# A two-layer streaming encoder on one core: S5 quarters, attention pairs and projections of the first mixer in one interleaved order, with the accumulator's memory lent to attention

## The chip, the cores and the metric

The kernel runs on one core of a Trainium2 chip, as one program. The time is device microseconds (us) of one execution. TensorE (PE in the profile, with PEld for its weight loads), VectorE (DVE), ScalarE (ACT) and GpSimd (POOL) compute; SyncE (SP) issues nearly all transfers.

## The reference, cut to what matters

Two requests are served in one step: 512 new frames of one stream, and 16 frames of each of 8 running streams, 640 rows of width 1024 in all. Two layers follow one another. Each has a half-weighted SwiGLU feed-forward part (FFN), a mixer and a second FFN, and after each of them a layer norm of ALPHA * x + sublayer(x). The change touches the first layer's mixer alone:

```python
proj = x @ w_in                      # (640 x 1024) @ (1024 x 2048): u | q | k | v, 512 columns each
ys, h_last = s5_recurrence(u, h0, a_bar, b_bar, c_mat)     # 32 groups, complex diagonal state of 64
y = ys + d_skip * u
g = gelu(y)
s5_out = g * sigmoid(g @ w_glu + b_glu)
# stick-breaking attention, 8 heads of 64, for each block of 128 queries
z = q @ k.T * 64 ** -0.5
sp = where(mask, softplus(z), 0)
w = where(mask, exp(log_sigmoid(z) - (reverse_cumsum(sp) - sp)), 0)
sb_out = w @ v
out = concatenate([s5_out, sb_out]) @ w_out
```

The 512 rows of the new stream attend causally to themselves. The 16 rows of each running stream attend to 256 cached keys and values and to their own rows. k, v and the last S5 states are outputs too.

## The kernel before, in words

The kernel is written in a framework that plans the order of each engine's instructions itself. Program order gives priorities; an instruction is put on its engine's queue when a plan with estimated durations says that its inputs and its buffer are ready, and so later work of the program can be queued between earlier work. Each queue then runs strictly in the planned order. Buffers come from pools with a fixed number of slots (`bufs`); pools of a closed block give their memory to those of the next.

All 640 columns of x, transposed, stand in SBUF as the sum of two parts, xh and xl, and every weight matrix is split in the same way when it arrives (`load_w` L106, `split` L94 and L95: a cast on ScalarE and a subtraction on VectorE). A product is three matmuls for each 128 rows of depth (`mm3`, L127). Weights are held in 11 units of 128 x 1024 fp32 (`UNITS`), two units for a load of 512 KB, behind four raw tiles that the DMAs fill. `yacc` (128 x 5 x 1024 fp32) is the residual accumulator: it holds x, and the projections out of FFN and mixer are added to it.

`mixer0` (from L604) runs in this order:

- u: four weights, eight column groups (`cm_proj`), copied to `g_` (L629).
- four S5 quarters (`s5_quarter`, L646 to L753): 128 of the 512 channels each. The tables m2, tt, et and rot come by DMA into buffers of their own; u is transposed twice (L661, L668), multiplied into the state inputs (L676), rotated and scanned on VectorE (L684 to L724), multiplied out (L730 with tt, L735 with et), transposed back (L743), and goes through a GELU made of exponentials (L748 to L753). The quarters use the four PSUM banks "b".
- v: four weights, five row tiles (L764), on the four banks "a".
- Then the block of S5 closes, and that of attention opens with new PSUM pools: three banks "a" for projections, one bank "o", and two tiles "z" of two banks each. `in_qk(p)` makes q and k of two heads (L932).
- Four pairs of heads. `attend(p, i)` works on query block i of 128 rows and its 128 (i + 1) keys, both heads in one z tile: scores (L838), mask (L841), softplus in four steps (clamp L827, two activations L82, maximum L830), a reverse running sum by a scan per head (L846), a subtraction (L848), an exponential (L82), transposes back into z (L853), a copy (L854) and the product with v into bank "o" (L857), which is copied over q at the end of the pair (L942). `sample(p)` does the running streams of that pair in one z tile and one bank "o" (L866 to L920), with cached keys and values by DMA (L883, L904).
- GLU of the S5 part (L963 to L966), the first half of the output projection (`out_half(0, t)`, L779, into yacc), and the second half with the layer norm, whose inputs are the attention results.

## Time and profile before

| | before |
|---|---|
| times of three runs | 2612.27, 2610.0, 2612.27 us, median 2612.27 |
| profiled execution, its own time | 2612.16 us |
| its span, first to last instruction | 2610.0 us |
| mean granted TensorE clock | 0.992 |
| busy in the span: PE, PEld, DVE, ACT, POOL | 2550.6, 2311.2, 2026.8, 1149.1, 239.2 us |
| S5 quarters | first transposes 483.3 us, first of the fourth quarter 532.0 us |
| v copied out of PSUM | 498.0 to 550.3 us (begin of the first and the last) |
| attention scores (L838) | 579.3 to 712.9 us (begin of the first and the last) |
| first half of the output added into yacc | from 671.1 us |

A line of the profile names the engine, the program line, the operation, what is written and read, the shape and the count, then busy time and mean duration of one, and after the second bar the idle time of the engine before it with what ended it. In the timeline the first two numbers are start and duration in us, and the bracket holds idle time before. In the table by stretches each engine has its busy time and its number of instructions; PEclk is the granted clock as a share of full speed. Ends of matmuls are modelled, so the ends of neighbours overlap by a fraction of a microsecond.

### The profile page before, as it was taken

What the parts mean: (1) busy time and instruction counts of PE and PEld (TensorE: products, weight loads), DVE (VectorE), ACT (ScalarE), POOL (GpSimd) and SP (SyncE); (2) the same over time, 40 slices, a digit from 0 to 9 for tenths busy, and PEclk for the clock granted to TensorE, in tenths of its full rate; (3) what the DMA queues carried; (4) which work ended last, traced back from release to release, by engine and by line L of the source; (5) the groups of instructions that cost most, each with busy time, mean ns of one, the idle gap of its engine ahead of it and who ended that gap; (6) DMA issues with size and microseconds to landing.
All of it is one profiled execution on the core that took longest, in us unless ns stands there. A gap on an engine that the chain in (4) does not pass through costs nothing. (4 is left out here: it accounts for less than half of the span.)

```text
span 2610.0 us, 41343 instructions
## 1 busy us (share of the span) xinstructions
PE 2550.6 (98%) x15673; PEld 2311.2 (89%) x15673; DVE 2026.8 (78%) x4074; ACT 1149.1 (44%) x2400; POOL 239.2 (9%) x356
## 2 busy tenths in 40 slices
PE   9999999999879999999999999999999999999998
PEld 8999999887559999999999999889989878898887
DVE  7898888667859777768976677877786789887778
ACT  4444444346524344334433343566565553343332
POOL 0000003010020000003000001311111150000001
PEclk9999999999979999999999999999999999999999
DMA  5233234542302232222222222456564622443432
GB/s 180 97 114 99 96 110 139 175 146 84 109 24 74 81 97 98 73 85 86 75 88 81 71 91 99 128 171 195 154 208 136 217 92 94 146 151 127 132 122 93
DMA packets 165751, 302.79 MB, mean 116 GB/s; under 512 B 19072, under 2 KB 89856, under 8 KB 165040
## 3 DMA queue, kind: packets, MB, share of 16 engines
q1 hardware_dynamic: 163792, 293.83, 35.0%
q0 software_dynamic: 1760, 6.33, 0.7%
q8 instruction: 123, 2.02, 0.3%
q14 instruction: 76, 0.62, 0.1%
HBM read 259.56 MB, written 40.54 MB: 115 GB/s over the span
## 5 line engine op out<-in xcount | busy, mean ns | idle before, releaser
L127 PE MATMUL bank<-w,h 128*128 128x512 f32 x2640 | 610.9, 391 | 0.0
L127 PEld LDWEIGHTS bank<-w,h 128*128 128x128 f32 x2640 | 492.5, 188 | 105.3 <-issue 3.4
L127 PE MATMUL bank<-xhi,w 128*128 128x256 f32 (+2 forms) x2528 | 556.6, 311 | 8.8 <-ACT w L94 5.7
L95 DVE TENSOR_TENSOR w<-raw,w 128x512 fp32r<-128x512 f32 x693 | 472.0, 692 | 101.9 <-ACT w L94 99.5
L340 PE MATMUL bank<-xhi,w 128*128 128x320 f32 x2432 | 540.1, 310 | 0.7 <-DVE w L95 0.3
L94 ACT CAST w<-raw 128x512 fp32r<-128x512 f32 x693 | 422.3, 620 | 254.8 <-PE bank L340 131.0
L127 PEld LDWEIGHTS bank<-xhi,w 128*128 128x128 f32 x2528 | 421.0, 188 | 21.7 <-issue 7.2
L340 PE MATMUL bank<-T,w 128*128 128x320 f32 x2736 | 425.6, 309 | 0.1
L340 PEld LDWEIGHTS bank<-xhi,w 128*128 128x128 f32 x2432 | 406.6, 188 | 7.1 <-issue 3.9
L340 PEld LDWEIGHTS bank<-T,w 128*128 128x128 f32 x2736 | 406.6, 188 | 0.4 <-DVE w L95 0.3
L127 PE MATMUL bank<-xlo,w 128*128 128x256 f32 (+2 forms) x1264 | 391.4, 310 | 1.7 <-DVE xlo L95 1.6
L340 PE MATMUL bank<-xlo,w 128*128 128x320 f32 x1216 | 375.5, 309 | 0.0
L94 ACT CAST w<-sw 128x512 fp32r<-128x512 f32 x228 | 137.8, 620 | 457.9 <-PE bank L127 276.7
L204 DVE SCALAR_TENSOR_TENSOR yacc<-bank,yacc 128x512 f32<-128x512 f32 x240 | 164.7, 688 | 213.6 <-PE bank L127 212.0
L127 PEld LDWEIGHTS bank<-xlo,w 128*128 128x128 f32 x1264 | 238.1, 188 | 3.8 <-DVE xlo L95 2.8
L340 PEld LDWEIGHTS bank<-xlo,w 128*128 128x128 f32 x1216 | 228.2, 188 | 0.0
L95 DVE TENSOR_TENSOR w<-sw,w 128x512 fp32r<-128x512 f32 x228 | 156.1, 685 | 11.8 <-ACT w L94 11.5
L152 POOL DMA_DIRECT2D w<-in_ln_gb_dram x12 | 6.9, 576 | 1236.8 <-DVE h L95 1217.1
L127 PE MATMUL bank<-w,og 128*128 128x512 f32 x432 | 105.3, 397 | 2.2 <-DVE og L1334 2.0
L94 ACT CAST h<-hf 128x320 fp32r<-128x320 f32 x160 | 73.3, 459 | 55.9 <-DVE hf L377 48.7
L127 PEld LDWEIGHTS bank<-w,og 128*128 128x128 f32 x432 | 79.5, 188 | 20.3 <-DVE og L1334 4.2
L127 PE MATMUL bank<-w,xhi 128*128 128x512 f32 x240 | 83.3, 412 | 1.1 <-DVE yacc L779 1.1
(392 smaller groups left out, 2877.0 us busy)
## 6 DMA issues: line engine op xcount, KB each, us to landing
raw<-in_w_gate_dram SPq DMA_DIRECT2D x88, 512.0 KB, 3.7
raw<-in_w_up_dram SPq DMA_DIRECT2D x88, 512.0 KB, 3.7
raw<-in_w_down_dram SPq DMA_DIRECT2D x88, 512.0 KB, 4.1
raw<-in_m_in_dram SPq DMA_DIRECT2D x52, 512.0 KB, 3.8
raw<-in_m_out_dram SPq DMA_DIRECT2D x24, 512.0 KB, 3.8
csb<-cs_d SPq DMA_DIRECT2D x20, 512.0 KB, 5.0
h<-in_ssd_h_dram SPq DMA_DIRECT2D x16, 512.0 KB, 5.8
h<-in_ssd_h_dram SPq DMA_DIRECT2D x32, 256.0 KB, 2.7
```

The lines of the kernel that those rows point to most:

```text
L94: nc.scalar.copy(hi, src)
L95: return nc.vector.tensor_tensor(lo, src, hi.bitcast(F32), op=ALU.subtract)
L127: state["pe"] = nc.tensor.matmul(ps, a, b, start=(k == 0), stop=(k == n - 1)).ins
L152: nc.gpsimd.dma_start(g_bc[j], bass.AP(tensor=I["ln_gb"].tensor, offset=I["ln_gb"].offset + (2 * n + j) * D, ap=[[0, 128], [1, D]]))
L204: state["acc"] = nc.vector.scalar_tensor_tensor(ya, pb, scale, ya, op0=ALU.mult, op1=ALU.add).ins
L340: nc.tensor.matmul(ps, A[p][:, a, k * 128:k * 128 + 128], B[p][b][:, k, :], start=(first and n == 0), stop=(n == 11), skip_group_check=True)
```

## The change

Nothing is computed differently but softplus, which was ln(1 + exp(min(z, 40))) with a maximum against z, and is max(z, 0) + ln(1 + exp(-|z|)): the clamp on VectorE gives way to an absolute value on ScalarE.

- The S5 quarters and the attention stand in one block. Order of the program: u; the accumulator written to DRAM; quarter 0; q and k of pair 0; v; then for p of 0, 1, 2: pair p, quarter p + 1, q and k of pair p + 1, sample p; then the accumulator read back; pair 3, sample 3; the splits of g and q; GLU and the output halves as before.
- `yacc` is written to DRAM (`y_d`) after u and read back after sample 2. Between, its five slices serve as attention's work buffers (`lent`): three in turn for e, two for S. Pair 3 uses five tiles p0 to p4 (`place`) that S5's intermediates share.
- S5's tables and its transposed u (ut, yt) use five of the 11 weight units (`flat_unit`) and no longer buffers of their own; et is loaded in two transfers.
- PSUM: two banks "a", two banks "b", two z tiles. Bank "o" is gone: products with v go into the first bank of the z tile, and are copied to q for each query block; `sample` uses its z tile alone.
- Query blocks 1 and 0 are done as one block of 384 columns for each head.

```diff
+        y_d = dram.tile([NT, 128, D], F32, name="y_d")
...
+        qk = {}
+
+        def load_qk(p):
+            for n in range(2):
+                qk[p, n] = load_w(I["m0_in"][4 + 2 * p + n])
+
+        def in_qk(p):
+            for n, sc in ((0, 0.125), (1, 1.0)):
+                t = keep.tile([128, T], F32, name="qk"[n] + "T", bufs=4 - n)
+                for h in range(2):
+                    o, L = HALVES[h]
+                    nc.scalar.mul(t[:, o:o + L], cm_proj(qk[p, n], h)[:, :L], sc)
+                qk[p, "qk"[n]] = t
+            nc.sync.dma_start(O["kT"][128 * p:128 * p + 128, :], qk[p, "k"])
...
-            wk = pool("m0_s5", 1, st, reuse_waits="tile")
+            wk = pool("m0_at", 1, st, reuse_waits="tile")
...
+            for t in range(NT):
+                nc.sync.dma_start(y_d[t], yacc[:, t, :])
+            banks[-1].close()
+            ctx_p = ExitStack()
+            psum(ctx_p, "m0a", a=2, b=2)
+            pools["z"] = pool("ps_m0a_z", 2, ctx_p, space=PSUM, reuse_waits="tile")
+
+            def bank_z():
+
+                return pools["z"].tile([128, 2, 512], F32, name="bank")
+
+            def flat_unit():
+                return unit(F32).rearrange("p a b -> p (a b)")
+
+            def place(n, *shape):
+                t = wk.tile([128, 1024], F32, name=n, bufs=1)[:, :math.prod(shape)]
+                return t.rearrange(f"p ({' '.join('abc'[:len(shape)])}) -> p {' '.join('abc'[:len(shape)])}",
+                                   **dict(zip("abc", shape)))
...
+                m2 = flat_unit()
+                nc.sync.dma_start(m2, s5d["m2"][j])
+                m2 = m2.rearrange("p (a r c) -> p a r c", a=4, r=2)
...
+                tt = flat_unit().rearrange("p (t c) -> p t c", t=8)
...
+                et = [flat_unit() for _ in range(2)]
+                for r in range(2):
+                    nc.sync.dma_start(et[r], s5d["e"][j][:, 1024 * r:1024 * r + 1024])
+                et = [t.rearrange("p (a c) -> p a c", a=4) for t in et]
...
+                ut = flat_unit().rearrange("p (g k c) -> p g k c", g=8, k=8)
...
+                uc = place("p0", 8, 80)
...
+                yt = ut.rearrange("p g k c -> p (g k c)").rearrange("p (t c) -> p t c", t=8)
...
-            for j in range(4):
-                s5_quarter(j)
...
-            psum(ctx_p, "m0a", a=3, o=1)
-            pools["z"] = pool("ps_m0a_z", 2, ctx_p, space=PSUM, reuse_waits="tile")
-            wk = pool("m0_at", 1, st, reuse_waits="tile")
...
+            def v_rev():
+                pr = bank_b()
+                nc.tensor.matmul(pr, anti, vt[:, 4, :], start=True, stop=True)
+                nc.scalar.copy(vrev, pr)
...
             def softplus_(e, z):
-                V.tensor_scalar_min(e, z, 40.0)
-                act_fn(e, e, AF.Exp)
+                nc.scalar.activation(e, z, AF.Abs)
+                act_fn(e, e, AF.Exp, scale=-1.0)
                 act_fn(e, e, AF.Ln, bias=1.0)
-                V.tensor_tensor(e, z, e, op=ALU.max)
-
+                V.scalar_tensor_tensor(e, z, 0.0, e, op0=ALU.max, op1=ALU.add)
+            turn = [0]
+            def lent(p):
+                n = turn[0]
+                turn[0] += 1
+                return [yacc[:, k, :].rearrange("p (h c) -> p h c", h=2) if p < 3 else place(f"p{k}", 2, 512)
+                        for k in (n % 3, 3 + n % 2)]
+            def attend(p, parts, qT, kT):
+                n = sum(128 * i + 128 for i, _ in parts)
                 z = bank_z()
+                for i, o in parts:
+                    for h in range(2):
+                        rows = slice(64 * h, 64 * h + 64)
+                        nc.tensor.matmul(z[:, h, o:o + 128 * i + 128], qT[rows, 128 * i:128 * i + 128],
+                                         kT[rows, :128 * i + 128], start=(o == 0), stop=False, skip_group_check=True)
+                for i, o in parts:
+                    for h in range(2):
+                        nc.tensor.matmul(z[:, h, o + 128 * i:o + 128 * i + 128], identb, negc,
+                                         start=False, stop=True, skip_group_check=True)
+                e, S = (t[:, :, :n] for t in lent(p))
+                softplus_(e, z[:, :, :n])
+                for i, o in parts:
+                    c = slice(o, o + 128 * i + 128)
+                    for h in range(2):
+                        V.tensor_tensor_scan(S[:, h, c][:, ::-1], onec[:, 0:1].to_broadcast([128, 128 * i + 128]),
+                                             e[:, h, c][:, ::-1], 0.0, op0=ALU.mult, op1=ALU.add)
+                V.tensor_tensor(S, z[:, :, :n], S, op=ALU.subtract)
+                act_fn(S, S, AF.Exp)
                 for h in range(2):
+                    for c in range(0, n, 128):
+                        nc.tensor.transpose(z[:, h, c:c + 128], S[:, h, c:c + 128], ident)
+                nc.scalar.copy(e, z[:, :, :n])
+                for m, (i, o) in enumerate(parts):
                     for j in range(i + 1):
+                        for h in range(2):
+                            nc.tensor.matmul(z[64 * h:64 * h + 64, 0, 128 * m:128 * m + 128],
+                                             vt[:, j, 128 * p + 64 * h:128 * p + 64 * h + 64],
+                                             e[:, h, o + 128 * j:o + 128 * j + 128],
+                                             start=(j == 0), stop=(j == i), skip_group_check=True)
+                    V.tensor_copy(qT[:, 128 * i:128 * i + 128], z[:, 0, 128 * m:128 * m + 128])
...
-                pk = bank("o")
                 zs = bank_z()
-                nc.tensor.transpose(pk[:, 0:128], kT[:, 512:640], ident)
...
+                sp, S = (t[:, :, :384] for t in lent(p))
...
+            def pair(p):
+                for parts in (((3, 0),), ((2, 0),), ((1, 0), (0, 256))):
+                    attend(p, parts, qk[p, "q"], qk[p, "k"])
+            s5_quarter(0)
+            load_qk(0)
             in_qk(0)
-            in_qk(1)
+            wv = [load_w(I["m0_v"][i]) for i in range(4)]
+            v_in()
+            v_rev()
+            for p in range(3):
+                pair(p)
+                s5_quarter(p + 1)
+                load_qk(p + 1)
+                in_qk(p + 1)
+                sample(p, qk[p, "q"], qk[p, "k"])
+            for t in range(NT):
+                nc.sync.dma_start(yacc[:, t, :], y_d[t])
+            for r in range(2):
+                nc.sync.dma_start(O["s5"][r], fin[:, r])
+            pair(3)
+            sample(3, qk[3, "q"], qk[3, "k"])
+            for m in range(4):
+                split(xh[:, m, :], xl[:, m, :], g_[m])
             for p in range(4):
-                qT, kT = qk[p, "q"], qk[p, "k"]
-                po = bank("o")
-                for i in range(4):
-                    attend(p, i, qT, kT, po)
-                V.tensor_copy(qT[:, 0:512], po)
-                sample(p, qT, kT)
-                if p < 2:
-                    in_qk(p + 2)
-                if p == 1:
-                    for m in range(4):
-                        split(xh[:, m, :], xl[:, m, :], g_[m])
-                    split(xh[:, 4, :], xl[:, 4, :], qk[0, "q"])
-                if p:
-                    split(xh[:, 4 + p, :], xl[:, 4 + p, :], qT)
+                split(xh[:, 4 + p, :], xl[:, 4 + p, :], qk[p, "q"])
```

More of the change, by code (lines that the diff above doesn't have):

```diff
@@ L619, in sigmoid_, with out_half @@
             act_fn(t, t, AF.Exp, scale=-1.0)
+        wo = {}
+        def out_half(k0, t):
+            ks = range(k0, k0 + 4)
+            for j in range(2):
+                pb = bank_a()
+                mm3(pb, [(xh[:, k, t * 128:t * 128 + 128], xl[:, k, t * 128:t * 128 + 128]) for k in ks],
+                    [w_j(wo[k], j) for k in ks])
+                ya = yacc[:, t, j * 512:j * 512 + 512]
+                V.scalar_tensor_tensor(ya, pb, 1.0 / ALPHA, ya, op0=ALU.mult, op1=ALU.add)
+        qk = {}
[10 more added lines that the diff above has]
+            nc.sync.dma_start(O["kT"][128 * p:128 * p + 128, :], qk[p, "k"])
         with ExitStack() as st:
-            wk = pool("m0_s5", 1, st, reuse_waits="tile")
+            wk = pool("m0_at", 1, st, reuse_waits="tile")
             w = {}
@@ L680, in s5_quarter @@
                 sn = rot[:, 1].rearrange("p (a c) -> p a c", c=64)
-                za, zb = (wk.tile([128, 4, 64], F32, name=n, bufs=1) for n in ("za", "zb"))
-                ta, tb = (wk.tile([128, 4, 64], F32, name=n, bufs=1) for n in ("ta", "tb"))
+                zt = place("p4", 4, 256)
+                za, zb, ta, tb = (zt[:, n].rearrange("p (a c) -> p a c", c=64) for n in range(4))
                 pr_, pi_ = sr[:, :, 0:64], si[:, :, 0:64]
@@ L738, in s5_quarter @@
                                    py[:80].rearrange("c g (t p) -> c g t p", p=16))
-                y = wk.tile([128, T], F32, name="y", bufs=1)
+                y = place("p1", T)
                 for hb in range(2):
@@ L744, in s5_quarter @@
                     V.tensor_copy(y.rearrange("p (c t) -> p t c", t=8)[:, 4 * hb:4 * hb + 4, :], pt)
-                g = wk.tile([128, T], F32, name="g", bufs=1)
+                g = place("p2", T)
                 act_fn(g, y, AF.Square)
@@ L821, in mixer0 @@
             nc.gpsimd.memset(qb, 0.0)
-            pr = bank("o")
-            nc.tensor.matmul(pr, anti, vt[:, 4, :], start=True, stop=True)
-            nc.scalar.copy(vrev, pr)
+            def v_rev():
+                pr = bank_b()
+                nc.tensor.matmul(pr, anti, vt[:, 4, :], start=True, stop=True)
+                nc.scalar.copy(vrev, pr)
             def softplus_(e, z):
-                V.tensor_scalar_min(e, z, 40.0)
-                act_fn(e, e, AF.Exp)
+                nc.scalar.activation(e, z, AF.Abs)
+                act_fn(e, e, AF.Exp, scale=-1.0)
@@ L829, in softplus_ @@
                 act_fn(e, e, AF.Ln, bias=1.0)
-                V.tensor_tensor(e, z, e, op=ALU.max)
-            def attend(p, i, qT, kT, po):
-                n = 128 * i + 128
-                z = bank_z()
-                for h in range(2):
-                    rows = slice(64 * h, 64 * h + 64)
-                    nc.tensor.matmul(z[:, h, :n], qT[rows, n - 128:n], kT[rows, :n],
-                                     start=True, stop=False, skip_group_check=True)
-                for h in range(2):
-                    nc.tensor.matmul(z[:, h, n - 128:n], identb, negc, start=False, stop=True, skip_group_check=True)
-                e = wk.tile([128, 2, 512], F32, name="es", bufs=4)
-                S = wk.tile([128, 2, 512], F32, name="S", bufs=2)
-                softplus_(e[:, :, :n], z[:, :, :n])
-                for h in range(2):
-                    V.tensor_tensor_scan(S[:, h, :n][:, ::-1], onec[:, 0:1].to_broadcast([128, n]),
-                                         e[:, h, :n][:, ::-1], 0.0, op0=ALU.mult, op1=ALU.add)
-                V.tensor_tensor(S[:, :, :n], z[:, :, :n], S[:, :, :n], op=ALU.subtract)
-                act_fn(S[:, :, :n], S[:, :, :n], AF.Exp)
-                for h in range(2):
-                    for j in range(i + 1):
-                        nc.tensor.transpose(z[:, h, 128 * j:128 * j + 128], S[:, h, 128 * j:128 * j + 128], ident)
-                nc.scalar.copy(e[:, :, :n], z[:, :, :n])
-                for j in range(i + 1):
-                    for h in range(2):
-                        nc.tensor.matmul(po[64 * h:64 * h + 64, n - 128:n],
-                                         vt[:, j, 128 * p + 64 * h:128 * p + 64 * h + 64],
-                                         e[:, h, 128 * j:128 * j + 128],
-                                         start=(j == 0), stop=(j == i), skip_group_check=True)
@@ L910, in sample @@
                             nc.tensor.matmul(po[32 * j:32 * j + 32, f], wT[:, f, 1 + k, 32 * j:32 * j + 32],
-                                             vcs[k][:, j, :], start=False, stop=(f == 1 and k == 1),
+                                             vcs[k][:, j, :], start=False, stop=(k == 1),
                                              skip_group_check=True)
-                nc.scalar.copy(pvs, po[:, 0:2])
-                pt = pk[:, :256]
+                nc.scalar.copy(pvs, po)
+                pt = zs[:, 0, 128:384]
                 for f in range(2):
```

72 lines of the change are left out of this document (19 added, 53 removed).

## The prediction, made before the changed kernel was built

> **What bounds the kernel now.** I read the page first, then the busy times by stretch, then the PE and DVE timelines of the first mixer (483.2 to 751.3 us).
>
> ```profile
> PE 2550.6 (98%) x15673; PEld 2311.2 (89%) x15673; DVE 2026.8 (78%) x4074; ACT 1149.1 (44%) x2400; POOL 239.2 (9%) x356
> ```
>
> ```profile
> core 0: us, PE busy (x) PEld busy (x) DVE busy (x) ACT busy (x) POOL busy (x), PEclk, DMA share, GB/s
> 483.20:557.00 73.80, 72.09 (x522) 57.28 (x521) 56.13 (x171) 29.85 (x49) 5.07 (x19) 1.00 0.47 153
> 557.00:579.20 22.20, 22.20 (x148) 21.56 (x146) 6.55 (x15) 6.81 (x14) 4.87 (x16) 1.00 0.46 146
> 579.20:713.90 134.70, 125.94 (x910) 93.96 (x909) 104.91 (x169) 81.65 (x151) 2.91 (x8) 1.00 0.29 90
> 713.90:751.30 37.40, 18.11 (x113) 11.08 (x112) 16.84 (x22) 10.48 (x16) 0.00 (x0) 0.57 0.18 62
> ```
>
> The whole execution is bound by TensorE: 59 us of 2610 are idle. Half of that idle time lies in the first mixer, and very unevenly. The S5 quarters with the V projection (first row) leave 73.80 - 72.09 = 1.7 us idle, the first q and k projections none, attention with filler 8.8 us, and the last stretch 37.40 - 18.11 = 19.3 us, at a mean granted clock of 0.57. The timeline shows that last stretch:
>
> ```profile
> 713.87 0.39 PE L127 MATMUL bank<-w,xhi 128*128 128x512 f32 x1
> 719.40 1.54 PE L853 MATMUL bank<-ident,S 128*128 128x128 f32 x6 [5.14 <-ACT S L82]
> ...
> 739.16 0.90 PE L897 MATMUL bank<-ident,es 128*128 128x128 f32 x3 [4.52 <-ACT es L82]
> ...
> 751.35 0.78 PE L127 MATMUL bank<-w,xhi 128*128 128x512 f32 x1
> ```
>
> From 713.9 to 751.3 no projection matmul (L127) is left. Only the chain of pair 3 and sample 3 runs. Why does attention last that long? VectorE's copies that end each pair (L942) and each sample (L920) show its beat:
>
> ```profile
> 605.22 0.69 DVE L942 COPY qT<-bank 128x512 f32<-128x512 f32 x1 [2.23 <-PE bank L857]
> 626.35 0.61 DVE L920 COPY qT<-bank 64x128 f32<-64x128 f32 x2 [0.47 <-PE bank L916]
> ...
> 667.83 0.60 DVE L920 COPY qT<-bank 64x128 f32<-64x128 f32 x2
> 709.19 0.60 DVE L920 COPY qT<-bank 64x128 f32<-64x128 f32 x2
> 729.94 0.69 DVE L942 COPY qT<-bank 128x512 f32<-128x512 f32 x1 [6.23 <-PE bank L857]
> 751.83 0.61 DVE L920 COPY qT<-bank 64x128 f32<-64x128 f32 x2 [3.18 <-PE bank L916]
> ```
>
> Pair, sample, pair, sample: 21.1 us from 605.22 to 626.35, and 41.5, 41.4 and 42.6 us from sample to sample. They are strictly in series, because both use the one bank "o". So attention is a chain of about 42 us per pair. It begins at 579 because its buffers open only after S5 and V, and by 713.9 all filler is eaten.
>
> **The change, part by part.** *What can be won.* The matmul work stays. Idle time 1.7 + 0 + 8.8 + 19.3 = 29.8 us; the 18.11 us busy in the last stretch would be 18.11 x 0.57 = 10.3 us at full clock, so 7.8 more. 37.6 us in all: with no idle time the stretch would last 268.1 - 37.6 = 230.5 us and end at 713.7.
>
> *Order and filler.* Attention can now begin once q and k of pair 0 stand. One 256-column and one 384-column group:
>
> ```profile
> 565.06 0.40 PE L127 MATMUL bank<-xhi,w 128*128 128x256 f32 x2
> ...
> 572.13 0.40 PE L127 MATMUL bank<-xhi,w 128*128 128x256 f32 x2
> ```
>
> take 7.07 us, so q and k of a pair 14.1 us, and GLU, eight groups of half that depth, 14.1 too. Three of the 512-column matmuls
>
> ```profile
> 753.42 0.63 PE L127 MATMUL bank<-w,xhi 128*128 128x512 f32 x2
> ...
> 754.12 0.63 PE L127 MATMUL bank<-w,xhi 128*128 128x512 f32 x2
> ```
>
> take 0.70 us, so V and the first output half, 120 of them each, 28 us each. One S5 quarter is
>
> ```profile
> 483.28 1.03 PE L661 MATMUL bank<-ident,g 128*80 128x128 f32 x8
> ...
> 498.31 1.04 PE L661 MATMUL bank<-ident,g 128*80 128x128 f32 x8
> ...
> 515.11 1.04 PE L661 MATMUL bank<-ident,g 128*80 128x128 f32 x8
> ```
>
> 16.8 us long as a chain (498.31 to 515.11). Its PE share comes from its groups over all four quarters, the largest
>
> ```profile
> L735 PE MATMUL bank<-et,hr 128*80 128x256 f32 x32 | 9.0, 384 | 1.1 <-issue 1.1
> L730 PE MATMUL bank<-tt,uc 128*80 128x128 f32 x64 | 8.6, 280 | 0.0
> L676 PE MATMUL bank<-uc,m 128*64 128x80 f32 x128 | 6.0, 239 | 0.0
> ```
>
> with another 9.0 for hi and 10.2 for the three transposes (L661, L668, L743): 42.8 / 4 = 10.7 us each, or some 8.3 where the overlapping ends of neighbours are counted once. The first pair can start at 483 + 14 + 10 = 507 instead of 579. V, three quarters, three q/k projections, GLU and the first output half lie beside the chain. Four pairs at today's 42 us would end at 507 + 168 = 675, and even from the end of V (535) at 703, before the 713.7 that PE needs. So PE, not the chain, should set the end.
>
> *New stalls.* Today's interleaving has 8.8 us in 134.7, 6.5%: PE reaches a transposition or a product slightly before ACT or DVE is ready,
>
> ```profile
> PE bank L853 <- ACT S L82: 3.5, 7, 0.9
> ```
>
> at most 0.9 us each time. At that rate the 207 us from 507 to 713.7 cost 207 x 0.065 / 0.935 = 14.4 us. Bounds: 1.7/73.8, the rate of today's S5 stretch, gives 5 us; twice today's rate gives 31. I take 14.4, the rate of the same kind of work.
>
> *Softplus and block merging.* One VectorE clamp becomes an Abs on ScalarE; blocks 1 and 0 go as one of width 768.
>
> ```profile
> L827 DVE TENSOR_SCALAR es<-bank 128x1024 f32<-128x1024 f32 x4 | 4.9, 1218 | 0.3 <-PE bank L841 0.3
> L830 DVE TENSOR_TENSOR es<-bank,es 128x1024 f32<-128x1024 f32 x4 | 4.8, 1208 | 0.0
> L846 DVE TENSOR_TENSOR_SCAN S<-onec,es 128x512 f32<-128x512 f32 x8 | 9.3, 1205 | 0.0
> L848 DVE TENSOR_TENSOR S<-bank,S 128x1024 f32<-128x1024 f32 x4 | 4.9, 1218 | 0.1
> L82 ACT ACTIVATE es<-es 128x1024 f32<-128x1024 f32 x8 | 8.5, 1058 | 1.2 <-DVE es L827 1.1
> L854 ACT COPY es<-bank 128x1024 f32<-128x1024 f32 x4 | 4.1, 1014 | 4.4 <-PE bank L853 4.4
> ```
>
> Abs is not in the trace; by the nearest rows it is 1.01 us (a PSUM read on ACT) to 1.22 us (the clamp), and I take 1.06. Then the widest block is 3 x 1.06 + 1.21 + 2 x 1.205 + 1.22 + 1.06 + 1.01, and about 1.1 us each of transposes and products: 12.3 us, as before within 0.2. VectorE has 56.1 + 6.6 + 104.9 + 16.8 = 184 us in the stretch and loses the clamps (4.9 for this form, 17.6 over all five forms), so about 168 of 250 us; ScalarE goes from 129 to some 141. Neither becomes the bound. The Trainium skill ("ScalarE: Activation LUTs", Rules for kernel authors) advises VectorE, not ScalarE, for max and min, which speaks against this move; the rows 1218 and 1058 disagree for this shape, and going by the page would add at most 0.2 us to a block. If Abs lay in another function set, two loads per block of
>
> ```profile
> L259 ACT ACT_TABLE_LOAD x1 | 1.3, 1283 | 0.0
> ```
>
> would add 2.6 us to each of 12 blocks and 8 sample halves: 51 us of ScalarE, 192 of 250, and 13 us per pair on a chain with slack. I take none. The same page (Table sets) says that abs stands in every set; no run here shows it yet.
>
> *Buffers.* Bank "o" is gone: its serial order ends, and two z tiles carry blocks and samples. About 33 us of blocks and 21 of a sample in two tiles are 27 us per pair, up to 42 with contention. The lent accumulator slices give three e and two S buffers, enough for two z tiles; a block waits for the buffer of the one two before it, which the z tile makes it do anyway. Projection banks go from 3 or 4 to 2: an evacuation of 0.4 to 0.7 us lies under the next group's 2.8 us or more. If the evacuation is late by half a microsecond in each of some 39 groups it is 20 us; I take 1.5 us. S5's banks go from 4 to 2, so its 2 us of L730 can no longer hide in the rotation: 2 us more chain, off the path.
>
> *DMAs.* Five writes and five reads of 512 KB, and S5's tables in weight units:
>
> ```profile
> raw<-in_m_out_dram SPq DMA_DIRECT2D x8, 512.0 KB, 3.6
> m<-m_d SPq DMA_DIRECT2D x4, 512.0 KB, 3.3
> et<-e_d SPq DMA_DIRECT2D x4, 1024.0 KB, 4.8
> ```
>
> The writes start when the norm before the mixer is through and run under the rest of the u projection, with S5's tables behind them on SP. Those tables, loaded early today, now wait for u's weight units, freed one after the other:
>
> ```profile
> 471.51 0.48 ACT L629 COPY g<-bank 128x384 f32<-128x384 f32 x1 [1.41 <-PE bank L127]
> ...
> 483.48 0.48 ACT L629 COPY g<-bank 128x384 f32<-128x384 f32 x1 [1.42 <-PE bank L127]
> ```
>
> The first quarter may start up to 5 us late with nothing else ready, and V's eight units wait for the quarter's five: 0 to 8 us, taken as 3 (q of pair 0 comes in between). The reload waits on SP for sample 2, ahead of sample 3's cache loads, the GLU weights and the output weights not yet fetched; GLU's 14 us covers its 3.6 us each. Taken as 0; without that cover it is the third rival.
>
> *Sum.* -37.6 + 14.4 + 3 + 1.5 = -18.7 us. The profiled execution took 2612.16 us (span 2610.0), and the median shown is 2612.27, equal within 0.01%. Forecast 2612.2 - 18.7 = **2593.5 us**.
>
> **Rivals.**
>
> *1. The order is taken up, but attention still ends last.* If S5's VectorE work (56.13 / 4 = 14 us a quarter) goes ahead of each pair's and the first products wait for V, then 535 + 3 x (42 + 14) + 42 = 745 instead of 751.3: **2606 us**, hardly to be told from no change. For it: VectorE serves both chains in order. Against: S5 stands behind the pair in the program, and VectorE is at two thirds.
>
> *2. Slower: weight units.* A quarter now holds five of the 11 units that weights use, V eight.
>
> ```profile
> SPq L106 <- DVE w L95: 148.4, 24, 35.8
> ```
>
> Weight loads already wait long for their buffers. If q/k weights get units only when a quarter releases its tables, each quarter runs with no filler, 16.8 - 8.3 = 8.5 us of idle PE (6 at the least); four cost 24 to 34 us. 2593.5 + 24 to 34 = 2617 to 2628, **2622 us**. It ends above today's time from the third bare quarter on (18.7 / 8.5 = 2.2). Against: 5 + 4 = 9 units fit beside each other.
>
> *3. The reload is late.* Then the first output half can't fill the last pair: 42 us of chain with about 15 of its own PE work and 14 of GLU leave 13 idle and some 5 of slow clock, 2593.5 + 18 = **2611 us**; half late, 2602.
>
> *4. Two banks lower the clock.* The stretch 579.2 to 713.9 kept 1.00 with 6.5% idle. If short waits on two banks brought a quarter of the 128 us of projections to half clock, 32 us: **2625 us**. The Trainium skill ("TensorE: Matmul & The Clock Gate", A second HAM failure mode: psum-queue depth-cycling) describes such a fall from cycling through PSUM banks. In this trace only gaps of 4.5 us and more stand beside a clock near a half.
>
> **How the numbers follow.** Forecast 0.55 (its own range 2582 to 2604, from stalls of 5 and 25 us in all); rival 1 0.10; rival 2 0.18; rival 3 0.12; rival 4 0.05. What can be told from no change is 0.2%, 5.2 us. Faster: 0.55, most of rival 3 and part of rival 1: 0.70. Same: 0.10. Slower: rivals 2 and 4 without their mild ends, 0.20. Range 2578 (stalls as rare as in today's S5 stretch) to 2622 (rival 2's middle).
>
> **What would show it.** Right: no stretch of several us without L127 before the second output half, a granted clock of 1.00 throughout the mixer, PE idle there below 20 us, the first attention score matmuls near 507 and not 579, samples overlapping the next pair, and one table load as before. Wrong: PE waits on the scalar casts of weights beside S5 (rival 2), a bare last pair with the reload landing late (rival 3), the clock below 1 beside dense projections (rival 4), or attention ending later than the first output half (rival 1).

## The result, and the profile after

The changed kernel took 2617.27 us (median of 11 runs) beside 2611.69 us for the kernel before (11 runs): a ratio of 1.0023, 95% interval 1.0013 to 1.0032. It is some 6 us slower, where 18.7 us less were forecast. Its profiled execution took 2619.16 us, span 2617.3.

The busy times of the page of the changed kernel, engine by engine:

```profile
PE 2557.5 (98%) x15673; PEld 2318.3 (89%) x15673; DVE 2010.1 (77%) x4054; ACT 1154.1 (44%) x2404; POOL 241.4 (9%) x356
```

PE is idle for 2617.3 - 2557.5 = 59.8 us. Before it was 2610.0 - 2550.6 = 59.4. Nothing of the idle time was won, and the same 15673 matmuls take 6.9 us longer in sum. Where does the idle time lie now? First the stretches of the kernel before (length, busy times of PE, PEld, DVE, ACT, POOL with instructions, granted clock, DMA share, GB/s), then of the changed one:

```profile
460.00:480.00 20.00, 19.61 (x128) 19.04 (x127) 11.30 (x23) 8.75 (x18) 0.47 (x1) 1.00 0.65 224
480.00:540.00 60.00, 58.52 (x444) 46.19 (x443) 44.08 (x136) 20.14 (x33) 2.47 (x13) 1.00 0.45 148
540.00:560.00 20.00, 19.78 (x118) 16.81 (x116) 14.98 (x42) 12.44 (x21) 3.96 (x11) 1.00 0.50 157
560.00:680.00 120.00, 112.48 (x817) 91.57 (x816) 85.86 (x139) 71.32 (x133) 4.67 (x15) 1.00 0.31 99
680.00:760.00 80.00, 59.47 (x368) 39.55 (x367) 45.42 (x71) 26.55 (x45) 1.75 (x4) 0.79 0.22 70
```

```profile
460.00:480.00 20.00, 15.56 (x104) 14.60 (x104) 8.70 (x22) 2.96 (x7) 6.50 (x21) 1.00 0.89 289
480.00:540.00 60.00, 58.53 (x350) 51.44 (x349) 20.09 (x54) 17.25 (x31) 1.96 (x6) 1.00 0.36 115
540.00:560.00 20.00, 13.34 (x79) 8.82 (x78) 11.12 (x14) 12.20 (x17) 0.00 (x0) 0.74 0.23 68
560.00:680.00 120.00, 113.12 (x911) 88.11 (x908) 92.09 (x208) 71.42 (x122) 3.61 (x12) 1.00 0.41 130
680.00:760.00 80.00, 68.69 (x400) 52.21 (x400) 49.66 (x85) 40.66 (x78) 2.74 (x4) 0.87 0.27 84
```

Reading length minus busy times clock as the loss of a stretch, before against after: 0.4 and 4.4 us at the end of u; 1.5 and 1.5; 0.2 and 10.1 at 540 to 560; 7.5 and 6.9; 33.0 and 20.2 in the tail. In sum 42.6 and 43.1. The mean clock of a stretch counts its idle time too: read in steps of half a microsecond, the tail of the kernel before loses 30.3 us, and the sums are 40.0 and 43.3. The tail is 10 us better by that reading, as the change meant, but the end of u (4.0 us) and 540 to 560 (9.9 us) together lose more than that. PE's timeline of the changed kernel shows the places, with the first scores (L874), the first output half (the row at 726.20) and the idle time with its releaser in brackets:

```profile
464.98 0.39 PE L127 MATMUL bank<-xhi,w 128*128 128x256 f32 x1 [1.75 <-DVE w L95]
472.52 0.44 PE L127 MATMUL bank<-xlo,w 128*128 128x384 f32 x1 [2.40 <-DVE xlo L95]
...
541.06 1.12 PE L874 MATMUL bank<-kT,qT 64*128 64x512 f32 x2
550.76 1.33 PE L719 MATMUL bank<-ident,w 80*128 80x80 f32 x8 [4.31 <-ACT w L713]
555.05 1.97 PE L892 MATMUL bank<-ident,yacc 128*128 128x128 f32 x8 [2.35 <-ACT yacc L82]
...
681.64 0.74 PE L127 MATMUL bank<-xhi,w 128*128 128x256 f32 x4 [2.29 <-ACT xhi L94]
692.17 0.39 PE L127 MATMUL bank<-xhi,w 128*128 128x256 f32 x1 [2.89 <-DVE gs L1001]
726.20 0.50 PE L127 MATMUL bank<-w,xhi 128*128 128x512 f32 x1 [0.80 <-DVE gs L1001]
```

Three things to explain: waits for VectorE in the u stage, a first pair that starts at 541 and is bare, and GLU waiting for its own clamp (`gs`), which lets the first output half begin only at 726, so that its last part runs alone behind attention (last sample's copy at 744.15).

### The profile page after: what moved, and what is told of

It reads as the page before. It is cut to its first block, busy times and chain, and to the rows that moved or that the text cites. A ratio compares the mean times of both kernels' runs of the same rounds, so it can differ in the third digit from the quotient of the medians.

```text
span 2617.3 us, 41376 instructions
## 1 busy us (share of the span) xinstructions
PE 2557.5 (98%) x15673; PEld 2318.3 (89%) x15673; DVE 2010.1 (77%) x4054; ACT 1154.1 (44%) x2404; POOL 241.4 (9%) x356
## 5 line engine op out<-in xcount | busy, mean ns | idle before, releaser
L127 PE MATMUL bank<-xhi,w 128*128 128x256 f32 (+2 forms) x2528 | 564.7, 314 | 16.8 <-ACT w L94 5.9
L95 DVE TENSOR_TENSOR h<-hf,h 128x320 fp32r<-128x320 f32 x160 | 76.9, 486 | 9.2 <-ACT h L94 9.0
```

The costliest lines, as they stand in the source:

```text
L95: return nc.vector.tensor_tensor(lo, src, hi.bitcast(F32), op=ALU.subtract)
L127: state["pe"] = nc.tensor.matmul(ps, a, b, start=(k == 0), stop=(k == n - 1)).ins
```

## The experiments

Each was timed beside the kernel before on one chip. To compare two of them I take the difference of their ratios to it, times 2611.7 us; with intervals of about 0.001 to each side a difference under some 3.7 us tells nothing. "Against after" is meant so.

**Mask set-up put back (e1).**

The set-up is issued only behind the last layer norm's power on GpSimd ("pow") and behind its last split on VectorE ("tr").

```diff
...
+            late_masks = ExitStack()
+            for n in ("pow", "tr"):
+                late_masks.enter_context(tc.issue_after(state[n]))
             identb = wk.tile([128, 128], BF16, name="identb", bufs=1)
...
+            late_masks.close()
```

> The changed kernel with one thing put back: the set-up of the masks, of anti and of the query buffer on VectorE and GpSimd is issued only behind the last layer norm of the u stage (behind its power on GpSimd and its last splits on VectorE). Theory (the set-up moved into the u stage and delays its last layer norm there): the gaps of 1.75 and 2.40 us of PE between 460 and 475 go, the u stage ends about 5 us earlier (last g copy near 484 instead of 488.7), and the time falls by about 5 us to 2612. Rival (the stage is late for another reason, S5's tables or the weight units): the gaps stay and the time stays at 2617.

Ratio 0.9999 [0.9990, 1.0008], 6.3 us less than after. In the kernel before, the set-up of this block came late on POOL, here the anti-diagonal matrix:

```profile
552.74 0.50 POOL L802 MEMSET anti<- 128x128 f32 x1 [21.55 <-DMA out_s_dram<-fin]
```

POOL and DVE of the changed kernel show what was in the way there:

```profile
460.00 1.02 POOL L837 TENSOR_SCALAR_AFFINE_SELECT mk<-mk 128x128 f32<-128x128 f32 x1
462.45 0.55 POOL L166 TENSOR_TENSOR rs<-rs,mhalf 128x1 f32<-128x1 f32 x1
```

```profile
463.04 1.28 DVE L179 SCALAR_TENSOR_TENSOR yacc<-yacc,rs,w 128x1024 f32<-128x1024 f32 x1 [1.51 <-POOL rs L166]
471.32 0.29 DVE L840 TENSOR_TENSOR mk<-mk 128x128 f32<-128x128 f32 x1 [2.08 <-POOL mk L837]
```

The masks stand ahead of the last norm's power (L166) on POOL, and VectorE, waiting for one mask (L840), holds up the splits behind it. With the set-up issued later the stretch reads

```profile
460.00:480.00 20.00, 19.55 (x128) 18.95 (x128) 8.42 (x22) 3.29 (x8) 7.93 (x22) 1.00 0.84 282
```

and the last copy of g starts at 483.96 instead of 488.72. The theory holds.

**The chain started ahead of V (e2).** `attend` is made a generator that stops behind the exponential, and pair 0's first two blocks are brought so far before V.

```diff
+            begun = list(pair(0))
+            for b in begun[:2]:
+                next(b)
             wv = [load_w(I["m0_v"][i]) for i in range(4)]
             v_in()
...
```

> The changed kernel with the first two blocks of pair 0, up to their exponentials, written ahead of V in the program; nothing else changes. Theory (V stands ahead of pair 0 in the order, so it runs as one dense block and the first pair is then left bare at 545 to 564): the first scores start near 513 instead of 541, VectorE is busy beside V, the two gaps of 4.31 and 2.35 us go, and the time falls by 8 to 10 us to about 2608. Rival (the first pair is bare because its products need V in any order, and filler is merely used up elsewhere): the gaps move and the time stays within 2 us of 2617.

Ratio 0.9959 [0.9947, 0.9972]: 16.7 us against after, nearly twice the expected. The stretches of 520 to 540 and 540 to 560, after and then in this kernel:

```profile
520.00:540.00 20.00, 20.00 (x89) 16.43 (x88) 0.00 (x0) 1.76 (x3) 0.00 (x0) 1.00 0.24 83
```

```profile
515.68 1.13 PE L874 MATMUL bank<-kT,qT 64*128 64x512 f32 x4
...
520.00:540.00 20.00, 20.00 (x89) 16.39 (x89) 8.21 (x8) 7.24 (x11) 0.00 (x0) 1.00 0.18 70
540.00:560.00 20.00, 19.80 (x169) 16.61 (x168) 9.47 (x20) 9.40 (x16) 0.00 (x0) 1.00 0.58 181
```

In the changed kernel V runs with VectorE at 0.00: PE is full, and nothing of the chain advances. Starting two blocks first fills that time, and the bare place goes. That it gave more than the 9.9 us lost there (10.1 less 0.2) fits the earlier chain also helping the tail: the loss from 680 to 760 is 80 - 74.79 x 0.96 = 8 us, from 20, while from 560 to 680 it is 120 - 108.36 x 0.99 = 13 us, up from 7. I have not separated these.

**Filler brought earlier instead (e3, and e17 with GLU's banks).**

```diff
             wv = [load_w(I["m0_v"][i]) for i in range(4)]
+            load_qk(1)
             v_in()
...
-                load_qk(p + 1)
+                if p:
+                    load_qk(p + 1)
```

> The changed kernel with the q and k weights of pair 1 loaded ahead of S5's tables of quarter 1 and ahead of the V matmuls. Theory (the bare stretch 545 to 564 lacks filler because the weights of pair 1 come too late): the PE gaps of 4.31 and 2.35 us shrink, the granted clock there is 1.00 instead of 0.74, and the time falls by 5 to 8 us to about 2611. Rival (the filler of the first pair is then missing later, in the tail where only GLU is left): the gaps of 545 to 564 go, but those of 679 to 726 grow, and the time stays within 2 us of 2617.

Ratio 1.0051 [1.0039, 1.0064]: 7.3 us slower than after, outside both expectations. The place itself was mended, and others opened:

```profile
540.00:560.00 20.00, 18.57 (x134) 13.58 (x134) 9.62 (x12) 10.90 (x16) 0.00 (x0) 1.00 0.67 221
580.00:600.00 20.00, 12.10 (x79) 7.97 (x79) 15.45 (x25) 14.20 (x24) 2.33 (x2) 0.69 0.38 111
...
680.00:700.00 20.00, 9.45 (x58) 5.19 (x52) 13.95 (x22) 11.62 (x19) 0.58 (x2) 0.67 0.49 160
```

> The run with the q and k weights of pair 1 ahead of V (2626.1) with GLU and the output halves on four banks and a second gate buffer besides. Theory (filler taken earlier is missing where pair 3 has GLU alone, and there two banks cannot deliver it: the 9 us lie in the tail): 2626 less 14.6 for the banks, less most of the 9 us, about 2603 to 2606, and no PE gap over 2 us behind 680. Rival (the loss lies beside sample 0, where S5's quarter 1 and the sample are left without projections): the gaps of 3.79 and 2.38 us between 585 and 597 stay, and the gains just add, 2611 to 2613.

Ratio 0.9995 [0.9986, 1.0004], 7.3 us against after. Four banks alone give 15.7 (e4, below) and 15.7 - 7.3 = 8.4, so the two simply add, the rival. The gap beside sample 0 is still there,

```profile
587.22 0.55 PE L937 MATMUL bank<-ident,yacc 128*128 128x128 f32 x3 [3.79 <-ACT yacc L82]
```

so part of the loss is beside sample 0, where S5's quarter 1 and the sample are left without projections. The tail has lost too: from 680 to 700 PE of e17 is busy 12.46 us at a clock of 0.76, where e4 with the same banks has 17.71 us at 1.00. Projections taken early are missing later; of the two, bringing the chain forward (e2) won.

**GLU's banks and gate buffer (e4 both, e5 the buffer, e14 the banks), and its place (e6).** The first pair of lines is in `out_half`, the second in GLU, the third is GLU's gate buffer; e6 has GLU written ahead of pair 3 instead.

```diff
-                pb = bank_a()
+                pb = bank("ab"[j])
...
-                    ps_ = bank_a()
+                    ps_ = bank("ab"[m % 2])
...
-                    s = wk.tile([128, 384], F32, name="gs", bufs=1)[:, :L]
+                    s = wk.tile([128, 384], F32, name="gs", bufs=2)[:, :L]
```

> The changed kernel with GLU's matmuls and both output halves taking the two pairs of banks in turn (four instead of two for them) and a second buffer for GLU's gate. Theory (GLU as the only filler from 679 to 726 is bound by its two banks and one gate buffer, which made PE wait 2.9 and 2.3 us): these waits go, the clock of 0.66 between 680 and 700 rises to 0.9 or more, and the time falls by 5 to 10 us to about 2610. Rival (GLU is late because attention's chain, ahead of it in the order, takes VectorE and ScalarE first): the waits stay and so does the time, 2617 within 2.

> The changed kernel with a second buffer for GLU's gate, and its two banks as they are. The run with four banks and the second gate buffer gained 14.6 us over the changed kernel. Theory (a gate buffer held through clamp, exponential, sigmoid and product, behind attention's own work, is what GLU waits for: PE's longest waits were on the DVE clamp that fills gs): most of that gain comes with the buffer alone, about 2606. Rival (the two banks bind, since a bank is held until the clamp has read it, buffer or no buffer): no change, 2617 within 3; then the banks carry the gain.

> The changed kernel with GLU and both output halves on four banks in turn, and one gate buffer as it is. With the buffer too it took 2602.6, with the buffer alone 2612.7. Theory (a bank is held until the clamp on VectorE has read it, and VectorE is late; with four banks PE goes on): 2603 to 2606, nearly the whole gain. Rival (the gate buffer binds once the banks do not, so both are needed): 2609 to 2613, and the two gains do not add up to the run with both.

> The changed kernel with GLU written ahead of pair 3 in the program, on its two banks and one gate buffer as they are. Theory (GLU waits because it has the last place in the order on VectorE and ScalarE): GLU goes as fast as its chain allows, the waits of 2.9 and 2.3 us between 680 and 700 go, and the time falls by 5 to 10 us, about as with four banks. Rival (two banks and one buffer bind in any order, and pair 3 is then held up by GLU's work ahead of it): the last pair ends later and the time stays at 2617 or rises by up to 5.

Both: 0.9963 [0.9950, 0.9975], 15.7 us against after. The buffer alone: 1.0003 [0.9994, 1.0012], 5.2. The banks alone: 0.9972 [0.9960, 0.9983], 13.3. GLU ahead of pair 3 on two banks: 0.9999 [0.9990, 1.0008], 6.3. The buffer's 5.2 us lie between its two expectations. The 6.3 us of the order are the 5 to 10 that its theory named, but not as much as four banks give. The banks carry most of it, and order helps without replacing them. PE's waits from 680 to 760, for the changed kernel (total, times, longest) and for e14:

```profile
PE bank L127 <- DVE gs L1001: 4.6, 3, 2.9
PE bank L127 <- ACT xhi L94: 2.3, 1, 2.3
```

```profile
PE bank L127 <- DVE gs L1001: 1.2, 1, 1.2
```

and the stretches where GLU is the only filler of the changed kernel, after and e14 (there the first output half starts at 705.45):

```profile
680.00:700.00 20.00, 14.02 (x89) 10.67 (x89) 13.16 (x20) 11.75 (x22) 1.57 (x2) 0.66 0.55 177
700.00:720.00 20.00, 16.50 (x106) 13.13 (x102) 13.76 (x25) 13.20 (x24) 0.00 (x0) 0.84 0.18 53
```

```profile
680.00:700.00 20.00, 17.74 (x142) 13.89 (x140) 17.16 (x30) 16.73 (x32) 2.38 (x2) 1.00 0.54 183
700.00:720.00 20.00, 17.74 (x122) 12.85 (x121) 16.48 (x30) 16.23 (x30) 0.00 (x0) 1.00 0.28 88
```

With two banks a bank stays taken until VectorE, which also works for attention, comes to the clamp (L1001). Four banks let PE go two groups further, and then VectorE and ScalarE do more in the same 20 us too.

**Bank "o" taken out of the kernel before (e7, and e13 without its own wait).**

```diff
-            psum(ctx_p, "m0a", a=3, o=1)
+            psum(ctx_p, "m0a", a=3)
...
-                        nc.tensor.matmul(po[64 * h:64 * h + 64, n - 128:n],
+                        nc.tensor.matmul(z[64 * h:64 * h + 64, 0, 0:128],
...
+                V.tensor_copy(qT[:, n - 128:n], z[:, 0, 0:128])
...
```

> The kernel before, with its order, buffers and softplus, but without bank o: each block's products go into a half of its own z tile, and a sample works in one z tile, so a sample can overlap the next pair. Three banks for projections instead of three and o. Theory of the prediction (the series pair, sample, pair, sample on bank o makes the chain of 42 us, and the chain sets the end at 751): the samples come closer than 41.5 us apart, the bare last stretch of 713.9 to 751.3 shrinks, and the time falls by 10 to 20 us to about 2597. Rival (as in the changed kernel, whose samples still came 41.5 and 44.2 us apart: the chain is not held by the bank but by VectorE's and ScalarE's work and the order on them): the cadence and the time stay, 2612 within 4.

> As the run without bank o (the kernel before otherwise), with the matmul that mirrors V's last tile issued behind the first q and k projections, so that it no longer makes PE wait for the anti-diagonal matrix. Theory of the prediction (bank o makes the series of pair and sample, and the chain sets the end): without that wait the gain comes out, 10 us or more, about 2600, with samples closer than 41 us apart. Rival (the series lies in the order of the work itself: a sample's steps stand behind the last block's in the program, whatever bank they use): the wait of 4.28 us goes, the samples stay 41 to 45 us apart, and the time is 2612 to 2617.

e7: 1.0039 [1.0025, 1.0053], with PE waiting 4.28 us for `anti` at 554.93, in front of the matmul that mirrors V's last tile. e13, without that wait: 1.0013 [1.0005, 1.0022], not faster. Its samples end at

```profile
626.55 0.59 DVE L918 COPY qT<-bank 64x128 f32<-64x128 f32 x2 [0.54 <-PE bank L914]
666.96 0.61 DVE L918 COPY qT<-bank 64x128 f32<-64x128 f32 x2 [0.52 <-PE bank L914]
710.00 0.61 DVE L918 COPY qT<-bank 64x128 f32<-64x128 f32 x2 [0.67 <-PE bank L914]
754.47 0.61 DVE L918 COPY qT<-bank 64x128 f32<-64x128 f32 x2 [6.67 <-PE bank L914]
```

40.4, 43.0 and 44.5 us apart. Its PE timeline at the end shows why nothing is gained (L835 scores, L854 products, L895 the sample's transposes):

```profile
710.26 0.92 PE L835 MATMUL bank<-kT,qT 64*128 64x384 f32 x4
711.32 1.13 PE L835 MATMUL bank<-kT,qT 64*128 64x512 f32 x4
...
728.70 1.97 PE L854 MATMUL bank<-es,vt 128*64 128x128 f32 x16 [0.89 <-ACT es L851]
...
738.33 0.90 PE L895 MATMUL bank<-ident,es 128*128 128x128 f32 x3 [4.59 <-ACT es L82]
746.31 0.90 PE L895 MATMUL bank<-ident,es 128*128 128x128 f32 x3 [4.52 <-ACT es L82]
```

Two blocks do go side by side in the two z tiles, but then both tiles are theirs, and the sample, two halves of 8 us one behind the other, still comes last.

**Softplus (e9) and the trip to DRAM (e10).**

```diff
-                nc.scalar.activation(e, z, AF.Abs)
-                act_fn(e, e, AF.Exp, scale=-1.0)
+                V.tensor_scalar_min(e, z, 40.0)
+                act_fn(e, e, AF.Exp)
                 act_fn(e, e, AF.Ln, bias=1.0)
-                V.scalar_tensor_tensor(e, z, 0.0, e, op0=ALU.max, op1=ALU.add)
+                V.tensor_tensor(e, z, e, op=ALU.max)
```

> The changed kernel with the softplus of before: a clamp and a max on VectorE instead of Abs on ScalarE, nothing else. 17.6 us of work go back to VectorE over the stretch. Theory of the prediction (neither engine is the bound and a block's chain is as long either way): 0, 2617 within 3. Rival (from 640 to 680 VectorE is busy for over 90% of the changed kernel's time, so it paces the pairs that share it with an S5 quarter): the last sample ends later by half of the added work or more and the time rises by 5 to 12 us to 2622 to 2629.

> The changed kernel without the accumulator's trip to DRAM: the five writes and five reads are left out, and with them the residual itself (attention's scratch is added instead), so only its time is of use. Theory of the prediction (writes hidden under the u projection, reload hidden under GLU): 2617 within 3. Rival (the writes are ahead of S5's tables on the queue, or the reload ahead of sample 3's caches and the GLU weights): 3 to 8 us faster, with earlier first S5 matmuls or fewer gaps between 675 and 726.

1.0024 [1.0015, 1.0034] and 1.0025 [1.0015, 1.0035]: neither can be told from after (1.0023). The 17.6 us of VectorE work cost nothing that can be told, and neither do writes and reload, so the rivals with 5 us or more are out; a cost under 3.7 us could hide.

**The edits together, and V or S5 moved on top (e8, e11, e12, e15, e16).** e8 joins e1, e2 and e4. The first diff is e12 on e8; e11 has the line ahead of V alone, and quarters 2 and 3 behind their pairs as they were. The second is e15 on e8 and e16 on e12, with pair 0's blocks taken from the short ones up.

```diff
+            s5_quarter(1)
             v_in()
...
             for p in range(3):
+                if p:
+                    s5_quarter(p + 1)
...
-                s5_quarter(p + 1)
```

```diff
-            v_in()
+            v_in((0, 1))
+            next(begun[0], 0)
+            next(begun[2])
+            v_in((2,))
+            next(begun[1], 0)
...
```

> The changed kernel with three edits together: mask set-up behind the last layer norm, the first two blocks of pair 0 ahead of V, and four banks with a second gate buffer for GLU and the output halves. Alone they gave -5.1, -15.8 and -14.6 us against the changed kernel. If the losses are separate places, as theory has it (u stage, bare first pair, tail), the gains add to 35.5 and the time is about 2582. If the filler kept by one edit is the same that another makes flow, as the run with the weights of pair 1 earlier suggests (its gaps came back 40 and 130 us later), the gains overlap: heads and GLU's banks together give no more than some 20, and the time is 2592 to 2597.

> The kernel of the three edits together (2588.8) with S5's quarter 1 written ahead of V as well, behind the two begun blocks. Its VectorE was busy 2.8 of 20 us from 520 to 540, beside V, and then 85 to 93% in four later stretches. Theory (within the mixer VectorE's idle time beside V is what later stands in the way of PE, so any VectorE work moved beside V is won back): VectorE is busy 10 us or more from 520 to 540, the gaps of 620 to 640 shrink, and the time falls by 4 to 8 us to about 2583. Rival (quarter 1 is the filler of pair 0's products, and it needs weight units that V holds until it is through): it cannot advance beside V, and the time stays at 2589 or rises by up to 5.

> As the run before, with quarters 2 and 3 also written ahead of pairs 1 and 2 instead of behind them. Theory (VectorE work early is good wherever PE has other filler): 2583 or 1 to 3 us better. Rival (attention is the longer chain, and S5's VectorE work ahead of it delays each pair by up to 14 us, while its own filler is used up): later samples and a time above that of the run before by 3 to 15 us.

> The kernel of the three edits (2588.8) with pair 0 in the order of growing blocks and V written tile by tile between them: blocks 1 and 0 begun, block 2 begun, V's tiles 0 and 1, the first products, block 3 begun, tile 2, and so on. Theory (V can be filler beside the chain, as the prediction had it, if the order lets it: VectorE's idle time beside V goes): VectorE is busy 10 us or more from 520 to 540 and the time falls by 4 to 8 us to about 2583. Rival (V's matmuls are ready at once and run as soon as PE is free, whatever is written between; the chain starts with the shorter blocks and has its longest one bare behind V): 2589 or up to 6 us slower.

> The same order of V and pair 0 on top of the fastest kernel so far (the three edits, and each S5 quarter written ahead of its pair, 2584.3). Theory (the VectorE time beside V is already taken by quarter 1 there, 6.3 us of 20 from 520 to 540): 1 to 4 us faster, about 2582. Rival (two chains already fill that time, and block 3 comes late): 2584 to 2590.

| kernel | median us | ratio to before | PE idle in the span |
|---|---|---|---|
| before | 2611.69 | 1 | 59.4 |
| after | 2617.27 | 1.0023 [1.0013, 1.0032] | 59.8 |
| e8, three edits | 2588.82 | 0.9913 [0.9900, 0.9927] | 41.7 |
| e11, quarter 1 ahead of V | 2590.47 | 0.9922 [0.9908, 0.9935] | 44.5 |
| e12, every quarter ahead of its pair | 2584.26 | 0.9900 [0.9886, 0.9913] | 39.6 |
| e15, V spread, on e8 | 2596.89 | 0.9942 [0.9930, 0.9954] | 47.1 |
| e16, V spread, on e12 | 2585.31 | 0.9896 [0.9881, 0.9911] | 40.5 |

The three edits alone sum to 6.3 + 16.7 + 15.7 = 38.7 us and give 28.7 together: separate places for the most part, with an overlap of 10 us, between the two expectations. Spreading V cost 7.6 us on e8, the rival and a little beyond its 6; on e12 it changed nothing that can be told, nor did quarter 1 ahead of V (e11 against e8). Both gave VectorE more to do beside V, from 520 to 540: 2.80 us in e8, 6.57 in e11, 7.85 in e15. That idle time, filled, was not won back. e12 is 26 us faster than the kernel before; that it beats e8 (3.4 us) is not certain. Its stretches:

```profile
460.00:480.00 20.00, 19.55 (x125) 19.11 (x125) 7.29 (x20) 3.27 (x7) 6.83 (x20) 1.00 0.78 266
480.00:540.00 60.00, 58.50 (x378) 48.87 (x377) 31.87 (x70) 26.66 (x43) 1.96 (x6) 1.00 0.38 118
540.00:560.00 20.00, 18.74 (x150) 15.03 (x149) 15.60 (x48) 9.62 (x14) 0.75 (x4) 1.00 0.56 177
560.00:680.00 120.00, 113.16 (x886) 91.35 (x885) 90.22 (x184) 80.18 (x143) 3.61 (x10) 0.99 0.39 126
680.00:760.00 80.00, 76.61 (x469) 57.93 (x468) 57.50 (x104) 37.86 (x64) 20.36 (x18) 1.00 0.30 96
```

Loss 0.5 + 1.5 + 1.3 + 8.0 + 3.4 = 14.7 us, from 43.1. The clock is at 0.99 or more in each of these stretches, with one fall inside the middle one (0.50 from 612.0 to 615.0). What remains lies mostly in the middle, 560 to 680: it lost 6.9 us in the changed kernel and still loses 8.0, though e12 moved the quarters there.

## Why the prediction was wrong, point by point

- **What can be won** (37.6 us): e12 shows that 26 us of it could be won. The order of the change took none of it.
- **"They are strictly in series, because both use the one bank 'o'"**: failed. Without that bank the beat stays (e13). That the z tiles and the place of a sample behind its pair keep the series is my reading of the PE lines of e13; no run separates the two. Nor did "four pairs at today's 42 us" hold in the changed kernel: from the first scores to the copy of the first sample are 76.6 us (541.06 to 617.67), with quarter 1 and q and k of pair 1 in between in the program; the next samples end 41.5, 44.2 and 40.8 us apart, the last at 744.15 and not by 703.
- **"The first pair can start at 507", with V "beside the chain"**: failed, and is one of the two large terms. The scores came at 541.06. V stood ahead of pair 0 in the program with every input ready, so it took PE whole while VectorE stood still. In the kernel before, V lay beside the running S5 quarters: VectorE was busy for 44.08 us from 480 to 540, and for 20.09 in the changed kernel. I took filler for something that lies beside a chain by itself; here it did so only where the chain was already running. The 507 itself was near: the first scores come at 515.68 in e2, and at 508.49 in e8, where the masks no longer delay u.
- **New stalls** (6.5%, 14.4 us): right where work was mixed (6.9 of 120 us, 5.7%), wrong as a rate for the whole, for it was taken from a stretch that always had q and k projections as filler, and the first pair had little and the last pair only GLU on two banks.
- **Two banks** (1.5 us): the term most under-sized. The banks alone are worth 13.3 us for GLU and the output halves, two thirds of the upper bound of 20. I priced an evacuation by its 0.4 to 0.7 us; it counts from when VectorE comes to it, and the wait was up to 2.9 us.
- **Not priced at all**: the mask set-up, 6.3 us. It stands in the block that was merged, so it moved with it, `anti` from 552.74 to 458.93, ahead of a layer norm on POOL and VectorE. I did not follow every instruction of the moved block.
- **Softplus**: 0 was right within what e9 can tell.

```profile
L852 ACT ACTIVATE yacc<-bank 128x1024 f32<-128x1024 f32 x3 | 3.1, 1018 | 0.7 <-PE bank L878 0.7
```

  Abs took 1.02 us where 1.06 was taken. There are eight table loads of 1283 ns before and after, and none of them in the first mixer. That abs stands in every function set, as the Trainium skill says ("ScalarE: Activation LUTs", Table sets), agrees with this trace. The merged blocks were not tried alone.
- **DMAs**: the trip to DRAM costs nothing that can be told (e10), and rival 3 (late reload, 9 to 18 us) is out with it. The 3 us for V's units and S5's tables were not separated.
- **Sum**: -18.7 forecast, +6.0 measured, 24.7 apart. V ahead of the chain (16.7), the banks (13.3 less 1.5) and the masks (6.3) are 34.8 alone, and less together, as in e8, whose 2588.8 us stands near the forecast of 2593.5.
- **Rivals**: rival 2 gave the sign and a time (2617 to 2628) that holds the measured one, but by luck: one stretch was bare, 540 to 560, not each quarter. Weights of pair 1 loaded earlier did fill that stretch (e3), and the time rose all the same. Rival 1 had the first products wait for V; in the trace the scores already did (541.06, behind V's last matmul), and the products came at 558.13, behind the chain's own copy (557.06). Rival 4 named the banks: with two of them the clock fell to 0.66 and 0.84 in the tail, and with four it stayed at 1.00 (e14). But it priced banks under dense projections, and these kept 1.00 on two banks from 560 to 680; the falls stand beside gaps of 1.6 to 2.9 us in the tail. The Trainium skill's fall from cycling through PSUM banks ("TensorE: Matmul & The Clock Gate", A second HAM failure mode: psum-queue depth-cycling) lays it to frequent short idling of PE between groups; the trace agrees in that the clock went down and up again three times between 682 and 721, in the stretch with these gaps.

What stays open: why the same matmuls take 6.9 us longer in sum. Little of it is the clock: at half clock 12.5 us of PE's time are lost from 460 to 760 against 9.8 before, but the kernel before loses another 1.7 later (from 2135.5 to 2139), so about 1 us is left. At a clock of 1.00, from 560 to 680, the mean of the 128x384 projections on `xhi` is 346 ns before and 351 after, and of the 128x256 ones 282 and 294; in e12 they are 345 and 288. How much of it is the mixing with short matmuls was not measured by itself.

## What to carry to other kernels

Filler has to be queued behind the start of the chain that it is to cover: a block of ready matmuls ahead of it runs dense, with the chain's engines idle beside it (VectorE 0.00 of 20 us here). What was won came from starting the chain early (e2); to put more VectorE work beside the same matmuls won nothing further (e11, e15). Price a buffer by how late its reader comes, not by how long the reader takes, above all where the same engine serves another chain. When blocks are merged, follow the small set-up instructions too: masks on GpSimd, moved forward with the block, sat in front of a layer norm.

## What the runs showed of the hardware that was not expected

The granted clock fell with smaller gaps than I had read from the trace of before ("only gaps of 4.5 us and more"). That reading held for the first mixer alone: in the same trace the clock is at 0.50 from 2135.5 to 2139, behind a gap of 1.65 us.

In steps of half a microsecond the clock of the first mixer is 1.00 or 0.50 in these traces, except in steps where it changes. A mean such as 0.66 is a mixture of the two, and with short gaps the low clock lies behind the gap, over work that is dense again. From 683 to 699.5 of the changed kernel, around the gaps that end at 681.64 (2.29 us) and 692.17 (2.89 us):

```profile
683.00:689.00 6.00, 5.66 (x28) 4.51 (x28) 5.04 (x7) 3.69 (x8) 1.28 (x1) 0.50 0.28 95
690.50:692.50 2.00, 0.33 (x2) 0.33 (x3) 2.00 (x4) 1.41 (x2) 0.00 (x0) 1.00 0.03 10
693.50:699.50 6.00, 6.00 (x48) 4.61 (x50) 1.79 (x4) 2.58 (x6) 0.00 (x0) 0.50 0.81 250
```

The falls last from some 3 us (e4, 471.0 to 474.5) to 34 us (before, 719 to 753). The length of a gap alone does not decide: the same two gaps of 1.75 and 2.40 us in the u stage left the clock at 1.00 in the changed kernel and brought the 3 us at 0.50 in e4. What decides between the two is not shown here.
